# The first branch's output adds on GpSimd, its last two units without GpSimd pairs, and the sums of down weights two units later

## The chip, the cores and the metric

The kernel runs on one core of a Trainium2 chip. The metric is the device time of one execution in microseconds (us); less is better. The engines that a core has are named as in the profile: PE (TensorE, the matrix engine), DVE (VectorE), ACT (ScalarE), POOL (GpSimd) and SP (SyncE, which here only issues DMAs). Each works through its own queue of instructions in order: an instruction that waits holds back all that stand behind it on its engine.

## The reference

One layer of a diffusion backbone over 1024 latent tokens and 256 context tokens, with a model width of 1024. What matters here is the attention; cut to its core:

```python
# A: 8 heads, windowed (+-128) with a sink logit; B: 8 heads, global. Both also see all 256 context keys.
def _sink_softmax(scores, sink):
    m = jnp.maximum(jnp.max(scores, axis=-1, keepdims=True), sink)
    e = jnp.exp(scores - m)
    return e / (jnp.sum(e, axis=-1, keepdims=True) + jnp.exp(sink - m))

out_a = _gqa_values(_sink_softmax(scores_a, sink), v_blk)      # per block of 128 queries
out_b = _gqa_values(jax.nn.softmax(scores_b, axis=-1), v_all)
merged = (g_a * (out_a @ w_branch_a) + g_b * (out_b @ w_branch_b)) @ w_out
```

Ahead of it stand the modulation and the projections to queries, keys, values and gates; behind it a LayerNorm, a SwiGLU feed-forward network with a convolution (weights up, gate and down), and a second LayerNorm.

## The kernel before, in words

The result has to be good to fp32, so the kernel splits fp32 operands in two parts that PE can take fast: a high part (a cast, line L83 or L81 on the helper `split`) and a low part (a subtraction, L86), and multiplies them as two or three matmuls that add up.

The stages in order: modulation and projections (to about 335 us), attention (to about 760 us), merge and output projection, the up and gate projections, the down projection. The down projection uses sums of blocks of the down weights; these sums are made in DRAM by DMAs alone, during the attention.

**Attention** is cut into 32 units. Unit `u` is a branch (0: windowed, units 0 to 15; 1: global, units 16 to 31), a block `i` of 128 queries and one of two groups `g` of four heads; the program's names carry it as `0_4_1` (branch, block, group). For each unit there are these steps:

- `qprep` (L476 to L488), two units ahead: POOL splits the queries into `qs` (L83, L86; one buffer for all units), PE transposes them (`qtr`, L483), ACT copies them out (L486), two DMAs swap halves.
- scores: for each head two or more matmuls into `s` (L493, L494; L528 adds the window's mask), then DVE's maximum (L538) and ACT's exponential (L505); `norm` (L562 to L573) ends the row sums `sm`.
- `rows` (L577 to L588): PE transposes the row sums (`str`), and three DMAs spread them over partitions (`rb`).
- values, one unit behind: for each key tile `n`, PE transposes the probabilities (`ptr`, L614), and they are split into `pth` and `ptl`. Most tiles go to ACT (the cast, L623) and DVE (the subtraction, L624). Tile 3 of each unit of branch 0, and tiles 2 and 6 of branch 1 (`POOL_LO`), are "pooled": ACT copies the tile to SBUF (`prw`, L620) and POOL does the cast and the subtraction (L83, L86). Then PE multiplies both parts with the values (`av`, L635 and L636).
- output, `out_step` (L638 to L655): ACT copies `av` to SBUF (`avs`, L641), POOL moves its upper half down (`up`, L643), two adds of 64x256 make `ot` (L647), POOL multiplies by `rb` (L650) and splits the result into `O` (L83, L86). The two adds run on DVE for branch 0 and for the last unit, on POOL for branch 1.

The loop over units at the end of the phase interleaves these steps; the order in which instructions stand on each engine is then set by a scheduler that weighs them with costs of its own. Branch projections (`fill`) are mixed in from unit 18 on. At the end of nine of the units, a table `DNS` calls `wd_sums`: SP loads a block of down weights into a DRAM tile `sd` (L683), and POOL issues a DMA that adds another block onto it (L685). It is POOL that waits there until the first has landed. Twelve such adds stand on POOL, in units 16 to 28. The sums are read much later, in the down projection.

Of the kernel before, what the change touches and what calls it, by code (L numbers as in the profile page):

```python
# [10 lines left out]
ALU = mybir.AluOpType  # L11
# [7 lines left out]
NT = 8  # L19
# [9 lines left out]
POOL_LO = (3,), (2, 6)  # L29
# [32 lines left out]
VOFF = 0.0  # L62
VSPAN = 1.0
VSC = 0, 1
DNS = {u0 + 2 * n + (u0 == 20): (n, j0, j1) for u0, j0, j1 in ((16, 0, 4), (20, 4, 8), (24, 8, 11)) for n in range(3)}


@with_exitstack
def layer_kernel(
# [6 lines left out]
    nc = tc.nc  # L76
    PSUM = bass.MemoryType.PSUM

    def split(src, hi, lo, hi_eng, lo_eng):
        if hi_eng is nc.scalar:  # L80
            nc.scalar.copy(hi, src)  # L81
        elif hi_eng is nc.gpsimd:
            nc.gpsimd.tensor_scalar(out=hi, in0=src, scalar1=1.0, scalar2=0.0, op0=ALU.mult, op1=ALU.add)  # L83
        else:
            hi_eng.tensor_copy(hi, src)
        lo_eng.tensor_tensor(out=lo, in0=src, in1=hi.bitcast(F32), op=ALU.subtract)  # L86
# [376 lines left out]
    class Unit:  # L463
# [141 lines left out]
        def value_steps(self):  # L605
            nm, kt = self.id, self.kt
            vh = self.br * 2 + self.g
            last = self.id == f"1_{NT - 1}_1"
            parts = {}

            def tr_step(n):
                tr = pt_tile(f"ptr{nm}_{n}")
                for h in range(4):
                    nc.tensor.transpose(tr[:, h * P:(h + 1) * P], self.pslice(h, n), ident)  # L614
                hi = att.tile([P, 512], R32, tag="pth", name=f"pth{nm}_{n}", bufs=4)
                lo = att.tile([P, 512], R32, tag="ptl", name=f"ptl{nm}_{n}", bufs=4)
                pooled = n in POOL_LO[self.br] and not last
                if pooled:
                    rw = att.tile([P, 512], F32, tag="ptr", name=f"prw{nm}_{n}", bufs=2)
                    nc.scalar.copy(rw, tr)  # L620
                    split(rw, hi, lo, nc.gpsimd, nc.gpsimd)
                else:
                    nc.scalar.copy(hi, tr)  # L623
                    nc.vector.tensor_tensor(out=lo, in0=tr, in1=hi.bitcast(F32), op=ALU.subtract)  # L624
                parts[n] = hi, lo
                return pooled

            def av_step(n):
                first = self.left == len(kt)
                self.left -= 1  # L630
                if first:
                    self.av = ps2.tile([P, 512], F32, tag="av", name=f"av{nm}")
                hi, lo = parts.pop(n)
                v = VT[kt[n] // 2][:, kt[n] % 2, vh]
                nc.tensor.matmul(self.av, v, hi, start=first, stop=False)  # L635
                nc.tensor.matmul(self.av, v, lo, start=False, stop=self.left == 0)  # L636

            def out_step():  # L638
                av = self.av
                avs = att.tile([P, 512], F32, tag="ptr", name=f"avs{nm}", bufs=2)  # L640
                nc.scalar.copy(avs, av)  # L641
                up = att.tile([HD, 512], F32, tag="up", name=f"up{nm}", bufs=1)
                nc.gpsimd.tensor_scalar(out=up, in0=avs[HD:P], scalar1=1.0, scalar2=0.0, op0=ALU.mult, op1=ALU.add)  # L643
                ot = att.tile([P, 2, P], F32, tag="ot", name=f"ot{nm}", bufs=1)
                oe = nc.gpsimd if self.br and not last else nc.vector
                for h in range(2):
                    oe.tensor_tensor(out=ot[h * HD:(h + 1) * HD],  # L647
                                     in0=avs[0:HD].rearrange("p (a b q) -> p a b q", b=2, q=P)[:, :, h],
                                     in1=up.rearrange("p (a b q) -> p a b q", b=2, q=P)[:, :, h], op=ALU.add)
                nc.gpsimd.tensor_tensor(out=ot, in0=ot, in1=self.rb, op=ALU.mult)  # L650
                hf = self.i // 4
                qs = slice((self.i % 4) * P, (self.i % 4 + 1) * P)
                split(ot, otile(self.br, hf, 0, self.g)[:, :, qs], otile(self.br, hf, 1, self.g)[:, :, qs],
                      nc.gpsimd, nc.gpsimd)

            def step(ns):
                pooled = [tr_step(n) for n in ns]
                for n, pl in zip(ns, pooled):
                    clk[0] += 1
                    avq.append((self, n, clk[0] + LAG[self.br] + (PLAG[self.br] if pl else 0)))  # L660
                    av_issue()

            self.left = len(kt)
            self.av_step, self.out_step = av_step, out_step
            g = 1 + self.br
            steps = [lambda n=n: step(range(n, n + g)) for n in range(0, len(kt), g)]
            steps.insert(3 if self.br else 2 if self.i else len(steps), self.rows)
            return steps

    tokens = []  # L670
    sd = {}

    def wd_sums(n, j0, j1):
        def a(r, c):
            return w_dn[c * NH + j0:c * NH + j1][:, :, 4 * r:4 * r + 4].rearrange("n p f q -> p n (f q)")

        def put(key, src, *more):
            tag = tokens.pop()
            t = dpool.tile([P, j1 - j0, HALF], F32, tag=tag, name=f"sd{key}_{j0}")
            for j in range(j0, j1):  # L680
                sd[key, j] = t[:, j - j0]
            sd[key] = t
            nc.sync.dma_start(t, src)  # L683
            for m in more:
                nc.gpsimd.dma_start(t, m, accum_op=ALU.add)  # L685

        if n == 0:
            put(1, a(1, 0), a(1, 1))
            put(3, a(0, 0), a(1, 0))
        elif n == 1:  # L690
            put(2, sd[1], a(0, 0))
        else:
            put(4, sd[2], a(0, 1))
# [130 lines left out]
    for n, (gi, k) in enumerate(order):  # L824
# [8 lines left out]
        if gi == "g":  # L833
            for hf in (0, 1):
                last = gate(k, hf)
# [50 lines left out]
    def otile(br, hf, hl, g):  # L886
        key = br, hf, hl, g
        if key not in O:
            O[key] = opool.tile([P, 2, HALF], R32, tag="O", name="O%d%d%d%d" % key, bufs=12)
        return O[key]  # L890
# [4 lines left out]
    def pt_tile(name, dt=F32):  # L895
        return ps2.tile([P, 512], dt, tag="pt", name=name, bufs=3)
# [17 lines left out]
    def av_issue(flush=False):  # L914
        while avq:
            u = avq[0][0]
            c = [e for e in avq if e[0] is u and (flush or e[2] <= clk[0])]
            if not c:
                return
            e = min(c, key=lambda e: e[2])  # L920
            avq.remove(e)
            u.av_step(e[1])
            if u.left == 0:
                u.out_step()
# [36 lines left out]
    def done(br, i, g):  # L961
        if g and i % 2:
            hput(f"Q{br}_{i - 1}")
        if g and i == NT - 1:
            hput(f"KL{br * 2}", f"KL{br * 2 + 1}")
# [4 lines left out]
    for u in range(nu + 1):  # L970
        vs, fs = [], []
        while vq and (vq[0] <= u - VL or vq[0] >= 16 or u >= 17):
            vs += units[vq.pop(0)].value_steps()
        ss = []
        if u < nu:
            ss = units[u].score_steps()
            if u + 2 < nu:
                ss.append(units[u + 2].qprep)
        if u == 31:
            first = branch_steps(1, w_b, (0, 1), att, (nc.gpsimd, nc.gpsimd), (0,))  # L980
            first[0]()
        for hf, (u0, u1) in enumerate(FILL):
            if u == u0:
                fill += branch_steps(0, w_a, (hf,), att, (nc.gpsimd, nc.gpsimd))
                ends = [n * (u1 - u0) / len(fill) for n in range(len(fill))]
            if u0 <= u < u1:
                fs = [fill.pop(0) for e in ends if u - u0 <= e < u - u0 + 1]
        if u < nu:
            ss = [units[u].context] + ss
        seq = []  # L990
        for lst, of, sp in ((ss, 0.0, SPAN[u >= 17]), (vs, VOFF, VSPAN), (fs, 0.0, 1.0)):
            for n, st_ in enumerate(lst):
                seq.append((of + sp * (n + 0.5) / len(lst), st_))
        for _, st_ in sorted(seq, key=lambda e: e[0]):
            st_()
        if u in DNS:
            wd_sums(*DNS[u])
        if u < nu:
            vq.append(u)
            done(units[u].br, units[u].i, units[u].g)  # L1000
# [86 lines left out]
    for f in range(2, KT):  # L1087
# [4 lines left out]
        for hs in halves:  # L1092
            n = HALF * len(hs)
# [239 lines left out]
    for f in (4, 6):  # L1333
        for si in (1, 2):
# [3 lines left out]
            elif f == 6:  # L1338
                (_, st), (_, dg), (_, ca), *ap = ln1(si)
                n = len(pend) - 4  # L1340
# [584 lines left out]
```

## Time and profile before

| What | Value |
|---|---|
| time, median of 3 runs | 1562.94 us (1562.52 to 1565.55) |
| time of the execution that was profiled | 1565.22 us |
| span of that execution in the profile | 1563.4 us |
| mean granted clock of PE | 0.995 of full speed |
| busy: PE, DVE, ACT, POOL | 98%, 76%, 52%, 50% of the span |
| attention | about 335 to 760 us |

How to read it: a row of the timeline has the start in us, the busy time in us, engine, line, operation, what it writes and reads, and how many instructions run together; in brackets stands how long the engine sat idle before it and which instruction released it. A row of a table of windows has, for each engine, its busy time in that stretch, then the granted clock of PE, the share of time in which the DMA engines were busy, and what they moved in GB/s. The times of one execution differ from the median of the runs by some us, so what the change adds or takes is worked out within the profiled execution.

### The profile page before, as it was taken

Reading aid. Unit: us, or ns where it says so; the run is one execution under the profiler, and the core shown is the slowest. Engines: PE = TensorE matmul, PEld = TensorE weight load, DVE = VectorE, ACT = ScalarE, POOL = GpSimd, SP = SyncE. Lnnn points to the kernel's source line nnn. Section 1 sums busy time; section 2 is a strip of 40 time slices with the busy share of each in tenths; the row PEclk is TensorE's granted clock in tenths of the full one; section 3 lists DMA queues with packets and bytes.
Section 4 is the critical chain, followed back from the end, with each engine's and each line's share of the span. In section 5 each row is a group of like instructions: output and inputs, shape, how many; then the busy total and the mean of one; then the engine's idle time right before and its main releaser. Section 6 shows DMA issues by size and latency. Waiting matters only on the chain.

```text
span 1563.4 us, 22286 instructions
## 1 busy us (share of the span) xinstructions
PE 1531.6 (98%) x7804; PEld 1282.2 (82%) x7804; DVE 1187.6 (76%) x1714; ACT 808.6 (52%) x1431; POOL 782.2 (50%) x795
## 2 busy tenths in 40 slices
PE   9999999999999999999999999999999999999997
PEld 7888888888877877877888997888888888888887
DVE  6677976548887777777774788888888888657884
ACT  5322223358887777777431673544444444435552
POOL 0356422526666777776332455666677764121121
PEclk9999999999999999999999999999999999999998
DMA  9776662322235666631550223233334446996721
GB/s 371 267 239 239 207 245 92 106 84 66 65 116 137 150 149 151 148 80 35 180 184 16 98 79 120 81 112 115 120 102 114 113 117 191 363 265 212 251 103 55
DMA packets 113105, 232.11 MB, mean 148 GB/s; under 512 B 13056, under 2 KB 27904, under 8 KB 112896
## 3 DMA queue, kind: packets, MB, share of 16 engines
q1 hardware_dynamic: 97760, 201.82, 38.4%
q0 software_dynamic: 10400, 20.19, 8.3%
q10 hardware_dynamic: 4832, 8.68, 1.5%
q8 instruction: 61, 1.00, 0.3%
q14 instruction: 52, 0.43, 0.1%
HBM read 179.45 MB, written 65.86 MB: 157 GB/s over the span
## 4 chain that ended last, share of the span: by engine, by line
PE 54%; DVE 3%; ACT 1%; issue 1%; POOL 0%; DVEq 0%; ACTq 0%
PE p L89 4%; PE p L90 4%; PE p L91 4%; PE b L89 2%; PE b L91 2%; PE b L90 2%; PE c L89 2%; PE c L91 2%; PE d L91 2%; PE d L89 2%; PE c L90 2%; PE d L90 2%; PE a L91 2%; PE a L89 2%; PE a L90 2%; PE y L91 2%
## 5 line engine op out<-in xcount | busy, mean ns | idle before, releaser
L624 DVE TENSOR_TENSOR ptl<-ptr,pth 128x512 fp32r<-128x512 f32 x190 | 126.2, 682 | 32.6 <-ACT pth L623 32.2
L623 ACT CAST pth<-ptr 128x512 fp32r<-128x512 f32 x190 | 108.0, 593 | 54.0 <-PE ptr L614 32.6
L86 DVE TENSOR_TENSOR ld<-rd,hd 128x1024 fp32r<-128x1024 f32 x77 | 94.9, 1249 | 50.2 <-ACT hd L81 48.1
L505 ACT ACTIVATE p<-p,nm 128x1024 f32<-128x1024 f32 (+2 forms) x128 | 125.9, 985 | 4.5 <-DVE p L538 4.3
L614 PE MATMUL ptr<-ident,p 128*128 128x128 f32 x816 | 122.4, 277 | 4.4 <-DVE ptl L624 3.2
L81 ACT CAST hd<-rd 128x1024 fp32r<-128x1024 f32 x77 | 79.5, 1050 | 81.1 <-PE p L91 55.1
L614 PEld LDWEIGHTS ptr<-ident,p 128*128 128x128 f32 x816 | 94.1, 141 | 25.6 <-DVE ptl L624 7.9
L86 POOL TENSOR_TENSOR wlg<-wg,whg 128x512 fp32r<-128x512 f32 x32 | 47.7, 1500 | 123.3 <-ACT whg L81 123.3
L635 PE MATMUL av<-pth,VT 128*128 128x512 f32 x236 | 104.6, 443 | 2.1 <-ACT avs L641 1.5
L89 PE MATMUL p<-hd 128*128 128x512 f32 x264 | 103.2, 391 | 0.0
L91 PE MATMUL p<-hd,ld 128*128 128x512 f32 x264 | 102.7, 389 | 0.0
L90 PE MATMUL p<-ld,hd 128*128 128x512 f32 x264 | 102.7, 389 | 0.0
L636 PE MATMUL av<-ptl,VT 128*128 128x512 f32 x236 | 98.1, 416 | 2.7 <-POOL ptl L86 2.7
L89 PE MATMUL g<-hh,whg 128*128 128x512 f32 x256 | 99.9, 390 | 0.0
L91 PE MATMUL g<-hh,wlg 128*128 128x512 f32 x256 | 99.7, 389 | 0.0
L90 PE MATMUL g<-hl,whg 128*128 128x512 f32 x256 | 99.6, 389 | 0.0
L538 DVE TENSOR_SCALAR_CACHE_REDUCE p<-s,cvt,nmc 128x1024 f32<-128x1024 f32 x64 | 83.2, 1316 | 8.8 <-PE s L494 7.7
L493 PE MATMUL s<-KL,q 128*128 128x512 f32 (+2 forms) x192 | 75.6, 394 | 5.3 <-ACT p_x L505 2.8
L787 ACT ACTIVATE sg<-g,bgc 128x512 f32<-128x512 f32 x32 | 22.0, 686 | 96.1 <-PE g L91 96.1
L494 PE MATMUL s<-KL,q 128*128 128x512 f32 (+2 forms) x192 | 71.6, 373 | 0.0
L81 ACT CAST wS<-s 128x512 fp32r<-128x512 f32 x76 | 45.3, 620 | 46.4 <-POOL s L1227 45.7
L81 ACT CAST wA<-ru 128x512 fp32r<-128x512 f32 x57 | 35.5, 623 | 62.4 <-PE d L91 33.8
(436 smaller groups left out, 5015.2 us busy)
## 6 DMA issues: line engine op xcount, KB each, us to landing
wml<-in_wmodT_dram SPq DMA_DIRECT2D x48, 512.0 KB
ru<-in_w_up_dram SPq DMA_DIRECT2D x38, 512.0 KB
rd<-td SPq DMA_DIRECT2D x55, 256.0 KB
rd<-sd SPq DMA_DIRECT2D x44, 256.0 KB
rd<-in_w_dn_dram SPq DMA_DIRECT2D x33, 256.0 KB
wm<-in_wmodT_dram SPq DMA_DIRECT2D x16, 512.0 KB
wg<-in_w_g_dram SPq DMA_DIRECT2D x32, 256.0 KB
sgd<-sg ACTq DMA_DIRECT2D x32, 256.0 KB
```

The source lines that it names most:

```text
L81: nc.scalar.copy(hi, src)
L86: lo_eng.tensor_tensor(out=lo, in0=src, in1=hi.bitcast(F32), op=ALU.subtract)
L89: nc.tensor.matmul(ps, a[0], b[0], start=start, stop=False, skip_group_check=resumed)
L90: nc.tensor.matmul(ps, a[0], b[1], start=False, stop=False, skip_group_check=resumed)
L91: nc.tensor.matmul(ps, a[1], b[0], start=False, stop=stop, skip_group_check=resumed)
L505: nc.scalar.activation(p, s, AF.Exp, bias=nm[:, h:h + 1], scale=scale, accum_out=sm[:, h:h + 1])
L538: nc.vector.tensor_scalar(out=p, in0=o, scalar1=self.qscale(nqs)[:, hs] if self.br else -1.0, scalar2=self.other[:, hs], op0=ALU.mult, op1 ...
L614: nc.tensor.transpose(tr[:, h * P:(h + 1) * P], self.pslice(h, n), ident)
L623: nc.scalar.copy(hi, tr)
L624: nc.vector.tensor_tensor(out=lo, in0=tr, in1=hi.bitcast(F32), op=ALU.subtract)
L635: nc.tensor.matmul(self.av, v, hi, start=first, stop=False)
L636: nc.tensor.matmul(self.av, v, lo, start=False, stop=self.left == 0)
```

## The change

Four edits, all in the attention phase:

1. `pooled` is false for block 7 of branch 0 (its last two units, `0_7_0` and `0_7_1`). Their tile 3 goes to ACT and DVE like the others.
2. The two adds into `ot` (L647) run on POOL for every unit but the last. Before, the 16 units of branch 0 had them on DVE.
3. `DNS` calls `wd_sums` two units later: at units 18, 20, 22, 23, 25, 27, 26, 28 and 30.
4. The accumulating DMAs are no longer issued in `wd_sums` at once, but put on a list, and issued on POOL at the end of the next unit.

```diff
-DNS = {u0 + 2 * n + (u0 == 20): (n, j0, j1) for u0, j0, j1 in ((16, 0, 4), (20, 4, 8), (24, 8, 11)) for n in range(3)}
+DNS = {u0 + 2 * n + (u0 == 22): (n, j0, j1) for u0, j0, j1 in ((18, 0, 4), (22, 4, 8), (26, 8, 11)) for n in range(3)}
...
-                pooled = n in POOL_LO[self.br] and not last
+                pooled = n in POOL_LO[self.br] and not last and self.id[:3] != f"0_{NT - 1}"
...
-                oe = nc.gpsimd if self.br and not last else nc.vector
+                oe = nc.vector if last else nc.gpsimd
...
+    adds = []
...
-            for m in more:
-                nc.gpsimd.dma_start(t, m, accum_op=ALU.add)
+            adds.extend((t, m) for m in more)
...
+        while adds:
+            t, m = adds.pop(0)
+            nc.gpsimd.dma_start(t, m, accum_op=ALU.add)
         if u in DNS:
             wd_sums(*DNS[u])
```

The scheduler gives several engines another order for it. On POOL, in the middle of branch 0, this is one cycle of before, from the query split of unit 0_4_1 to that of 0_5_0 (`qs` the split queries, `up`, `ot` and `O` the output of unit 0_2_0, `pth` and `ptl` the pooled tile 3 of unit 0_2_1):

```order
L83 TENSOR_SCALAR qs0_4_1_3957<-Q0_4_1588 128x4x64
L643 TENSOR_SCALAR up0_2_0_3812<-avs0_2_0_3810 64x512
L86 TENSOR_TENSOR qs0_4_1_3957<-Q0_4_1588,qs0_4_1_3957 128x4x64
L83 TENSOR_SCALAR pth0_2_1_3_3843<-prw0_2_1_3_3845 128x512
L650 TENSOR_TENSOR ot0_2_0_3814<-ot0_2_0_3814,rb0_2_0_3650 128x256
L86 TENSOR_TENSOR ptl0_2_1_3_3844<-prw0_2_1_3_3845,pth0_2_1_3_3843 128x512
L83 TENSOR_SCALAR O0000_3305<-ot0_2_0_3814 128x2x128
L86 TENSOR_TENSOR O0010_3306<-ot0_2_0_3814,O0000_3305 128x2x128
L83 TENSOR_SCALAR qs0_5_0_4089<-Q0_4_1588 128x4x64
```

And this is the same cycle on POOL after the change:

```order
L83 TENSOR_SCALAR qs0_4_1_3957<-Q0_4_1588 128x4x64
L643 TENSOR_SCALAR up0_2_0_3812<-avs0_2_0_3810 64x512
L86 TENSOR_TENSOR qs0_4_1_3957<-Q0_4_1588,qs0_4_1_3957 128x4x64
L647 TENSOR_TENSOR ot0_2_0_3814<-avs0_2_0_3810,up0_2_0_3812 64x256 x2
L650 TENSOR_TENSOR ot0_2_0_3814<-ot0_2_0_3814,rb0_2_0_3650 128x256
L83 TENSOR_SCALAR O0000_3305<-ot0_2_0_3814 128x2x128
L86 TENSOR_TENSOR O0010_3306<-ot0_2_0_3814,O0000_3305 128x2x128
L83 TENSOR_SCALAR pth0_2_1_3_3843<-prw0_2_1_3_3845 128x512
L86 TENSOR_TENSOR ptl0_2_1_3_3844<-prw0_2_1_3_3845,pth0_2_1_3_3843 128x512
L83 TENSOR_SCALAR qs0_5_0_4089<-Q0_4_1588 128x4x64
```

The two adds are new, and the pooled pair `pth`, `ptl` has gone from the middle of the cycle to its end, behind the whole output of the unit before. Ten cycles in a row, from the output of unit 0_1_0 to that of 0_5_1, stand like this; behind them come two cycles of another order.

On PE, before, the part of the same cycle from the use of the first pooled part (`pth0_2_1_3`) to the transpose of the next queries (`qtr0_4_1`) is this, `ptr` being transposes of unit 0_3_0 and `s` scores of unit 0_3_1:

```order
L635 MATMUL av0_2_1_3849<-pth0_2_1_3_3843,VT4_2139 128x512
L614 MATMUL ptr0_3_0_2_3929<-ident_58,p0_3_0_0_3750 128x128
...
L636 MATMUL av0_2_1_3849<-ptl0_2_1_3_3844,VT4_2139 128x512
L635 MATMUL av0_2_1_3849<-pth0_2_1_4_3857,VT4_2139 128x512
L493 MATMUL s0_3_1_2_3903<-KL1_2131,q10_3_1_3701 128x384
...
L636 MATMUL av0_2_1_3849<-ptl0_2_1_4_3858,VT4_2139 128x512
L483 MATMUL qtr0_4_1_3960<-identr_59,qs0_4_1_3957 128x128 x4
```

After the change the same instructions stand so:

```order
L635 MATMUL av0_2_1_3849<-pth0_2_1_3_3843,VT4_2139 128x512
L636 MATMUL av0_2_1_3849<-ptl0_2_1_3_3844,VT4_2139 128x512
L614 MATMUL ptr0_3_0_2_3929<-ident_58,p0_3_0_0_3750 128x128
...
L635 MATMUL av0_2_1_3849<-pth0_2_1_4_3857,VT4_2139 128x512
L636 MATMUL av0_2_1_3849<-ptl0_2_1_4_3858,VT4_2139 128x512
L483 MATMUL qtr0_4_1_3960<-identr_59,qs0_4_1_3957 128x128 x4
```

The five score matmuls of `s0_3_1_2` now stand ahead of `str0_3_0` and `pth0_2_1_3`; between the use of `ptl0_2_1_3` and the query transposes only four transposes and two matmuls are left. In both orders `qtr0_4_1` stands behind the use of the pooled low part.

On POOL, where branch 0 ends, before: the output of unit 0_7_0 with a DMA add (`sd1_0`) inside it, that of 0_7_1 behind it, and among them pooled pairs of branch 1:

```order
L643 TENSOR_SCALAR up0_7_0_5172<-avs0_7_0_5170 64x512
L685 DMA sd1_0_5183<-in_w_dn_dram 512x1x512
L650 TENSOR_TENSOR ot0_7_0_5174<-ot0_7_0_5174,rb0_7_0_4974 128x256
L83 TENSOR_SCALAR pth1_0_0_2_5244<-prw1_0_0_2_5246 128x512
L83 TENSOR_SCALAR O0100_4346<-ot0_7_0_5174 128x2x128
L86 TENSOR_TENSOR O0110_4347<-ot0_7_0_5174,O0100_4346 128x2x128
L86 TENSOR_TENSOR ptl1_0_0_2_5245<-prw1_0_0_2_5246,pth1_0_0_2_5244 128x512
L643 TENSOR_SCALAR up0_7_1_5263<-avs0_7_1_5261 64x512
L650 TENSOR_TENSOR ot0_7_1_5265<-ot0_7_1_5265,rb0_7_1_5112 128x256
```

And after, from the same instruction on:

```order
L643 TENSOR_SCALAR up0_7_0_5146<-avs0_7_0_5144 64x512
L647 TENSOR_TENSOR ot0_7_0_5148<-avs0_7_0_5144,up0_7_0_5146 64x256 x2
L650 TENSOR_TENSOR ot0_7_0_5148<-ot0_7_0_5148,rb0_7_0_4974 128x256
L83 TENSOR_SCALAR O0100_4346<-ot0_7_0_5148 128x2x128
L86 TENSOR_TENSOR O0110_4347<-ot0_7_0_5148,O0100_4346 128x2x128
...
L83 TENSOR_SCALAR pth1_0_0_2_5234<-prw1_0_0_2_5236 128x512
L643 TENSOR_SCALAR up0_7_1_5253<-avs0_7_1_5251 64x512
L86 TENSOR_TENSOR ptl1_0_0_2_5235<-prw1_0_0_2_5236,pth1_0_0_2_5234 128x512
```

No DMA add stands there any more, and ahead of this piece the pooled pair of unit 0_7_1 is gone from POOL too.

## The prediction

> **What bounds the kernel now.** I read the page first, for the busy shares:
>
> ```profile
> PE 1531.6 (98%) x7804; PEld 1282.2 (82%) x7804; DVE 1187.6 (76%) x1714; ACT 808.6 (52%) x1431; POOL 782.2 (50%) x795
> ```
>
> PE is the bound. Work that moves between the other engines counts only where PE waits for it, and POOL, at 50%, looks free. A share over the whole span says little, so I cut the attention into stretches with the table of windows:
>
> ```profile
> 390.00:420.00 30.00, 29.99 (x203) 25.89 (x202) 25.87 (x63) 27.29 (x66) 19.27 (x29) 1.00 0.25 67
> 465.00:500.00 35.00, 31.12 (x171) 24.28 (x170) 26.21 (x42) 26.45 (x60) 22.94 (x36) 0.95 0.59 129
> 482.08:485.49 3.41, 1.22 (x6) 0.72 (x7) 2.30 (x5) 0.00 (x0) 2.13 (x5) 1.00 1.07 195
> 485.49:488.90 3.41, 3.41 (x16) 2.92 (x17) 3.41 (x6) 2.01 (x4) 3.21 (x5) 0.50 0.02 4
> ```
>
> After each stretch's length stand the busy times of PE, its weight loads, DVE, ACT and POOL, then the granted clock. In the middle of branch 0 (390 to 420) PE has no gap. Where branch 0 hands over to branch 1 (465 to 500) PE loses some 4 us to waits, and right after a stretch with PE busy 1.22 of 3.41 us, it runs 3.41 us at half clock. So the change can win at the handover, and in branch 0 it can only lose. What it would lose there I looked up in one cycle of POOL's timeline:
>
> ```profile
> 399.45 0.41 POOL L83 TENSOR_SCALAR qs<-Q 128x256 fp32r<-128x256 f32 x1 [1.46 <-PE qtr L483]
> 399.94 0.61 POOL L643 TENSOR_SCALAR up<-avs 64x512 f32<-64x512 f32 x1
> 400.63 0.74 POOL L86 TENSOR_TENSOR qs<-Q,qs 128x256 fp32r<-128x256 f32 x1
> 402.42 0.62 POOL L83 TENSOR_SCALAR pth<-prw 128x512 fp32r<-128x512 f32 x1 [1.04 <-ACT prw L620]
> 403.00 0.74 POOL L650 TENSOR_TENSOR ot<-ot,rb 128x256 f32<-128x256 f32 x1
> 403.70 1.29 POOL L86 TENSOR_TENSOR ptl<-prw,pth 128x512 fp32r<-128x512 f32 x1
> 404.96 0.40 POOL L83 TENSOR_SCALAR O<-ot 128x256 fp32r<-128x256 f32 x1
> 405.44 0.74 POOL L86 TENSOR_TENSOR O<-ot,O 128x256 fp32r<-128x256 f32 x1
> 407.66 0.41 POOL L83 TENSOR_SCALAR qs<-Q 128x256 fp32r<-128x256 f32 x1 [1.48 <-PE qtr L483]
> ```
>
> A cycle takes 407.66 − 399.45 = 8.21 us, and POOL idles 1.48 + 1.04 = 2.5 us of it. PE's part of the same cycle:
>
> ```profile
> 405.20 0.66 PE L614 MATMUL ptr<-ident,p 128*128 128x128 f32 x4
> 405.62 0.48 PE L636 MATMUL av<-ptl,VT 128*128 128x512 f32 x1
> 405.94 0.40 PE L635 MATMUL av<-pth,VT 128*128 128x512 f32 x1
> 406.17 0.34 PE L493 MATMUL s<-KL,q 128*128 128x384 f32 x1
> ...
> 406.88 0.39 PE L636 MATMUL av<-ptl,VT 128*128 128x512 f32 x1
> 407.11 0.46 PE L483 MATMUL qtr<-identr,qs 128*128 128x128 f32 x4
> ```
>
> The `ptl` of 403.70 is done at 404.99, and PE takes it at 405.62, after 0.63 us of slack and without a wait. There is a ring: POOL's cast into `qs` waits for `qtr` of the unit before (one buffer), `qtr` stands in PE's queue behind the use of `ptl`, and `ptl` stands in POOL's queue behind the cast. Its length sets a floor under the cycle. Now it is 403.70 + 1.29 − 399.45 = 5.54 us on POOL plus 407.66 − 405.62 = 2.04 on PE and back, 7.6 in all, against the 8.2 of PE's own work. It does not bind.
>
> **The change part by part.** *Adds on POOL, branch 0.* What they cost per instruction, from the rows of their line:
>
> ```profile
> L647 DVE TENSOR_TENSOR ot<-avs,up x34: 388/418/862, 353.3 to 758.4; 64x256 f32<-64x256 f32 x34
> L647 POOL TENSOR_TENSOR ot<-avs,up x30: 717/732/755, 500.1 to 750.8; 64x256 f32<-64x256 f32 x30
> ```
>
> DVE saves 2 × 0.418 = 0.84 us a unit, which is worth nothing where PE has no gap. POOL pays 2 × 0.732 = 1.46. By busy time that fits into the 2.5 us of idle; but the new order puts both adds, the multiplication and the split of `O` ahead of the pooled pair, so all of it goes into the ring. Branch 1 already has this piece, in the same order:
>
> ```profile
> 500.07 1.52 POOL L647 TENSOR_TENSOR ot<-avs,up 64x256 f32<-64x256 f32 x2
> ...
> 504.38 1.30 POOL L86 TENSOR_TENSOR ptl<-prw,pth 128x512 fp32r<-128x512 f32 x1
> ```
>
> From the first add to the end of `ptl` it is 504.38 + 1.30 − 500.07 = 5.61 us. Ahead of it stand the cast, `up` and the low part of `qs`: 400.63 − 399.45 = 1.18, and about 0.70 from the start of the last to the next start (as 403.70 − 403.00 for an instruction as long). That is 7.49 on POOL. On PE the five score matmuls (406.88 − 406.17 = 0.71) are gone from behind `ptl`, and four transposes (405.62 − 405.20 = 0.42) stand there instead: 2.04 − 0.71 + 0.42 = 1.75. I add 0.06 for the hand from POOL to PE, which now waits (at 464.63 below). The ring is 7.49 + 0.06 + 1.75 = 9.30 us, so the cycle grows by 9.30 − 8.2 = 1.1, as a wait of PE for `ptl`. The ten cycles in the new order run, in the trace of before, from
>
> ```profile
> 366.26 0.41 POOL L83 TENSOR_SCALAR qs<-Q 128x256 fp32r<-128x256 f32 x1 [0.98 <-PE qtr L483]
> ...
> 440.44 0.41 POOL L83 TENSOR_SCALAR qs<-Q 128x256 fp32r<-128x256 f32 x1 [1.46 <-PE qtr L483]
> 449.45 0.41 POOL L83 TENSOR_SCALAR qs<-Q 128x256 fp32r<-128x256 f32 x1 [2.29 <-PE qtr L483]
> ```
>
> to the last of these (eight rows left out). The tenth takes 449.45 − 440.44 = 9.01 us already and hides most of the ring; the nine ahead of it, (440.44 − 366.26) / 9 = 8.24 each, pay: 9 × 1.10 = **+9.9**. If POOL ran gapless (7.07 us, the sum of the busy times in these rows with the adds), the ring would be 8.88 and the term +6; a ring of 9.4 gives +11. The tenth and the cycle behind it, which has another order: 0 to +1.1, taken as **+0.5**, the middle, no row being nearer.
>
> The Trainium skill's "GPSIMD Engine Reference", section "Engine selection", gives elementwise adds of two inputs to VectorE, with GpSimd about two times slower: it speaks against this edit. The rows here have 0.732 against 0.418, 1.75 times; by the page's factor two adds would be 1.67 instead of 1.46 us, and the term, by that estimate, +11.8.
>
> *The start of branch 0.* There the adds on DVE do hold PE up once:
>
> ```profile
> 353.30 0.42 DVE L647 TENSOR_TENSOR ot<-avs,up 64x256 f32<-64x256 f32 x1 [2.67 <-POOL up L643]
> ...
> 354.60 0.27 PE L577 MATMUL str<-ident,sm 128*4 128x128 f32 x1 [1.08 <-DVE sm L573]
> 355.28 0.44 PE L493 MATMUL s<-KL,q 128*128 128x384 f32 x1 [0.42 <-DVE p L538]
> ```
>
> DVE stood behind `up`, and the row sums and a maximum behind it. Without the adds the 1.08 + 0.42 us go: **−1.5**, at worst 0 if POOL, now with the adds, is late for something else there.
>
> *The handover: no pairs of units 14 and 15, no DMA adds, no adds on DVE.* PE, POOL and DVE of that stretch:
>
> ```profile
> 464.63 0.50 PE L636 MATMUL av<-ptl,VT 128*128 128x512 f32 x1 [1.44 <-POOL ptl L86]
> 482.47 0.50 PE L636 MATMUL av<-ptl,VT 128*128 128x512 f32 x1 [0.62 <-POOL ptl L86]
> 484.77 1.64 PE L614 MATMUL ptr<-ident,p 128*128 128x128 f32 x8 [1.80 <-DVE ptl L624]
> ...
> 477.40 1.18 POOL L685 DMA_DIRECT2D sd<-in_w_dn_dram  x1 [1.89 <-DMA sd<-in_w_dn_dram]
> ...
> 482.50 0.61 POOL L643 TENSOR_SCALAR up<-avs 64x512 f32<-64x512 f32 x1
> ...
> 483.15 0.85 DVE L647 TENSOR_TENSOR ot<-avs,up 64x256 f32<-64x256 f32 x2 [3.38 <-POOL up L643]
> 484.03 1.29 DVE L624 TENSOR_TENSOR ptl<-ptr,pth 128x512 fp32r<-128x512 f32 x2
> ```
>
> This is a chain: POOL waits 1.89 us for a block of down weights and issues the add for 1.18; 3.07 us late, `ptl` comes 0.62 too late for PE; `up` stands behind it, DVE waits 3.38 for `up`, two `ptl` stand behind that, and PE waits 1.80. The wait at 464.63 is for the pair of unit 0_7_0. All three have lost their cause: 1.44 + 0.62 + 1.80 = 3.86. The half clock behind them costs 3.41 / 2 = 1.7 more and should not come, since the share of 1.22 in 3.41 that stands ahead of it rises. Together −5.6 if nothing else gets late. Something will: the two pairs go to DVE and ACT (the low part is 1.29 us for two there, and 26.21 of 35 us were busy), and POOL's adds come before its first pairs of branch 1. I keep four fifths, **−4.5**; the bounds are −5.6 and −2.
>
> The Trainium skill's "TensorE: Matmul & The Clock Gate", section "What's actually happening", has the clock fall after a window of about 3.4 us in which PE idles. The trace shows 0.50 for just 3.41 us, but behind a window with 1.22 us of work, so here it was not a whole window without work. By the page's words the fall had a cause that the change need not touch, and this term would be −2.8.
>
> *The sums in units 18 to 30.* Moved, not removed. Their rows on POOL:
>
> ```profile
> L685 POOL DMA_DIRECT2D sd<-in_w_dn_dram x12: 1085/1122/1375, 465.7 to 692.3; - x12
>   DMA sd<-in_w_dn_dram: 3.6, 2
> ```
>
> The twelve cost POOL 1.12 us each before and after; the waits for loads (3.6 us in two places) shrink, as a unit now lies between load and add. What stands behind a waiting add on POOL is its pooled pairs, for which PE waits; only the one at 477.40 was seen to reach PE (above). SP's loads are issued as before, two units later, and what they make is read only in the down projection, long after the attention. **0 ± 1**.
>
> *Sum.* +9.9 + 0.5 − 1.5 − 4.5 + 0 = **+4.4 us**, so the profiled execution's 1565.22 would be 1569.6, and the median, 2.28 lower, 1562.94 + 4.4 = **1567.3**.
>
> **The rivals.** *POOL's slack takes the adds (faster).* The cycle stays at 8.2 and only the gains are left: 0 − 1.5 − 4.5 = −6, 1556.9. It speaks for it that POOL would be busy 7.2 of 8.2 us. The point that decides: the stretch from the cast to the end of `ptl` must be at most 8.2 − 1.75 − 0.06 = 6.39 us, 1.1 less than I count and less than the 7.07 of its instructions alone, unless PE reaches `qtr` by less than 1.75. I see no room for that, but I take these rows from two places of the trace, and the ring's closing depends on the one buffer of `qs`. 0.2.
>
> *The ring binds half as hard (no change).* If the instructions abut better and each cycle grows by 0.5 to 0.7, a loss of 4.5 to 6.3 with the +0.5 behind it meets gains of 6: −1 to +0.8, about 1563. It speaks for it that the gapless sum gives +6. 0.24.
>
> *The half clock stays (slower still).* If at the handover another wait lets PE work only a third of some window, the 3.41 us at 0.50 come again, and the sum is 1.7 higher: +6.1, 1569.0. Against it: no pooled pair and no DMA add of POOL's is left at that place. The Trainium skill's rule above would give the same, for another reason. 0.1.
>
> *The ring's waits bring the clock down (much slower).* A wait of 1.1 us in 9.3 leaves PE busy 88%. The fall came behind 36%, and the 1.44 us at 464.63 brought none. Once a cycle it would cost 9 × 1.7 = +15, 1583. 0.02.
>
> *The forecast* itself: 0.44.
>
> **How the numbers follow.** A measurement of this kernel can tell about 0.2% from no change, 3.1 us. Slower holds the forecast and the two cases with the clock, 0.56, less 0.04 for a forecast that comes out under 3.1 us: 0.52. Same: those 0.04 and 0.21 of the half-hard ring, 0.25. Faster: the slack and the rest of the half-hard ring, 0.23. The low end is the slack's 1556.9. For the high end I take the ring at +11, the cycle behind at +1.1, −1.5 and −2 for the gains, and 1 for the sums: +9.6, 1572.5. Within the slower cases but the last it is 1566 to 1572.5.
>
> **What would show it.** In the trace of after: between 366 and 450 the casts into `qs` some 9.3 us apart, POOL without idle time between them but for one wait for `qtr`, and PE waiting 1 us a cycle at L636 for POOL's `ptl`; no such waits and 8.2 us would make me wrong at the main step. At the handover no half clock, no wait for `sd` on POOL, and PE waiting under 1.2 us in all; the end of attention some 4 us later. If the start still shows 1.08 at `str`, that term is wrong. If the loss is in branch 1 (500 to 760), the cause is one that I priced at nothing.

## The result, and the profile after

| Kernel | Median | Ratio to before, 95% interval |
|---|---|---|
| before (6 runs) | 1563.43 us | |
| the change (6 runs) | 1568.63 us | 1.0033 [1.0020, 1.0046] |

The change makes the kernel slower by about 5.2 us, 3.1 to 7.2. The profiled execution of after has a span of 1567.7 us, 4.3 more than before's 1563.4. The page's first row and the table of windows, for the same stretches as in the prediction and for two around 740 us (columns as there):

```profile
PE 1534.7 (98%) x7804; PEld 1284.0 (82%) x7804; DVE 1177.2 (75%) x1684; ACT 807.9 (52%) x1431; POOL 806.4 (51%) x823
```

```profile
390.00:420.00 30.00, 26.88 (x175) 22.58 (x173) 21.63 (x51) 22.93 (x55) 22.68 (x33) 1.00 0.21 58
465.00:500.00 35.00, 34.41 (x212) 27.80 (x213) 30.54 (x53) 31.24 (x75) 27.16 (x46) 1.00 0.31 95
...
736.50:739.91 3.41, 1.75 (x9) 1.18 (x9) 2.43 (x5) 2.90 (x10) 0.45 (x1) 1.00 1.08 195
739.91:743.33 3.42, 3.42 (x13) 2.92 (x12) 2.56 (x4) 3.37 (x6) 2.60 (x4) 0.50 0.02 3
```

The shares of the page have hardly moved. The windows have: in the middle of branch 0 PE now loses 3.1 of 30 us where it lost nothing, at the handover it loses 0.6 of 35 where it lost 3.9, and the half clock of 3.41 us is gone from 485 us and has come at 739.9. One cycle of POOL after the change, and PE's use of the pooled low part in it:

```profile
403.46 0.41 POOL L83 TENSOR_SCALAR qs<-Q 128x256 fp32r<-128x256 f32 x1 [1.84 <-PE qtr L483]
...
405.35 1.53 POOL L647 TENSOR_TENSOR ot<-avs,up 64x256 f32<-64x256 f32 x2
...
409.67 1.27 POOL L86 TENSOR_TENSOR ptl<-prw,pth 128x512 fp32r<-128x512 f32 x1
412.79 0.41 POOL L83 TENSOR_SCALAR qs<-Q 128x256 fp32r<-128x256 f32 x1 [1.84 <-PE qtr L483]
```

```profile
411.00 0.50 PE L636 MATMUL av<-ptl,VT 128*128 128x512 f32 x1 [0.85 <-POOL ptl L86]
```

POOL's work of a cycle has no gap but the wait for `qtr`, and PE waits 0.85 us for `ptl`. The cycle is 412.79 − 403.46 = 9.33 us. It consists of 409.67 + 1.27 − 403.46 = 7.48 on POOL, 0.06 to PE, and 412.79 − 411.00 = 1.79 on PE and back.

To see where the 4.3 us come from, I compare the starts of like instructions, here POOL's casts into `qs`, in after:

```profile
366.10 0.41 POOL L83 TENSOR_SCALAR qs<-Q 128x256 fp32r<-128x256 f32 x1 [0.55 <-PE qtr L483]
...
450.15 0.41 POOL L83 TENSOR_SCALAR qs<-Q 128x256 fp32r<-128x256 f32 x1 [1.85 <-PE qtr L483]
459.05 0.40 POOL L83 TENSOR_SCALAR qs<-Q 128x256 fp32r<-128x256 f32 x1 [1.41 <-PE qtr L483]
469.19 0.40 POOL L83 TENSOR_SCALAR qs<-Q 128x256 fp32r<-128x256 f32 x1 [1.86 <-PE qtr L483]
...
510.74 0.41 POOL L83 TENSOR_SCALAR qs<-Q 128x256 fp32r<-128x256 f32 x1 [0.90 <-PE qtr L483]
```

and in before, where the counterparts of the last two are

```profile
457.87 0.40 POOL L83 TENSOR_SCALAR qs<-Q 128x256 fp32r<-128x256 f32 x1 [0.89 <-PE qtr L483]
...
506.57 0.41 POOL L83 TENSOR_SCALAR qs<-Q 128x256 fp32r<-128x256 f32 x1 [0.89 <-PE qtr L483]
```

Later on I take waits that PE has in both traces, first before, then after:

```profile
744.95 0.33 PE L614 MATMUL ptr<-ident,p 128*128 128x128 f32 x1 [0.48 <-DVE ptl L624]
...
971.20 0.47 PE L89 MATMUL c<-T13h,wS 128*128 128x512 f32 x1 [1.75 <-DVE c L1390]
```

```profile
750.32 0.33 PE L614 MATMUL ptr<-ident,p 128*128 128x128 f32 x1 [0.48 <-DVE ptl L624]
...
975.45 0.47 PE L89 MATMUL c<-T13h,wS 128*128 128x512 f32 x1 [0.63 <-DVE c L1393]
```

| Stretch (term) | after's lead or lag at its end | what the stretch cost | predicted |
|---|---|---|---|
| start of branch 0, to 366 | −0.16 | −0.2 | −1.5 |
| nine cycles, to before's 440.44 | +9.71 | +9.9 | +9.9 |
| tenth cycle and the one behind it, to 457.87 | +11.32 | +1.6 | +0.5 |
| handover, to 506.57 | +4.17 | −7.2 | −4.5 |
| branch 1, to 744.95 | +5.37 | +1.2 | 0 |
| rest, to 971.20 and the end | +4.25, +4.3 | −1.1 | not named |

The last row is no work of the change as far as the runs show: this wait at the wide matmuls was 1.75 us in before and 0.63 in after; in the twelve kernels below it was 0.62 to 0.64 in nine, 1.75 in two and 2.03 in one.

The marks are POOL's casts, and PE's queue stands in another order around two of them, so some of PE's work falls into another row of the table. Up to the first mark PE does 145 matmuls in before and 140 in after; the five that it does later are score matmuls of one head, 0.71 us by the rows of the prediction:

```profile
343.90:366.26 22.36, 20.86 (x145) 18.54 (x145) 18.11 (x45) 17.98 (x45) 14.03 (x20) 1.00 0.24 55
...
343.90:366.10 22.20, 20.65 (x140) 17.75 (x140) 16.94 (x41) 17.29 (x43) 16.88 (x25) 1.00 0.23 55
```

And ahead of the handover's first mark, six matmuls `s_x` (scores with the context) stand behind the query transposes in before (first two rows) and ahead of them in after (last two rows, 468.64 − 467.85 = 0.79 us):

```profile
457.24 0.54 PE L483 MATMUL qtr<-identr,qs 128*128 128x128 f32 x4
457.91 0.39 PE L493 MATMUL s_x<-KC,q 128*128 128x256 f32 x1
...
467.85 0.36 PE L493 MATMUL s_x<-KC,q 128*128 128x256 f32 x1
...
468.64 0.45 PE L483 MATMUL qtr<-identr,qs 128*128 128x128 f32 x4
```

For like work the start cost about +0.5 instead of −0.2, the nine cycles +9.2, the two behind them +0.8 and the handover −6.4. The sum stays the same.

### The profile page after: what moved, and what is told of

Its sections match the earlier page's. It is cut to its first block, busy times and chain, and to the rows that moved or that the text cites. A ratio compares the mean times of both kernels' runs of the same rounds, so it can differ in the third digit from the quotient of the medians.

```text
span 1567.7 us, 22275 instructions
## 1 busy us (share of the span) xinstructions
PE 1534.7 (98%) x7804; PEld 1284.0 (82%) x7804; DVE 1177.2 (75%) x1684; ACT 807.9 (52%) x1431; POOL 806.4 (51%) x823
## 4 chain that ended last, share of the span: by engine, by line
PE 54%; DVE 3%; ACT 1%; issue 1%; POOL 0%; DVEq 0%; ACTq 0%
PE p L89 4%; PE p L91 4%; PE p L90 4%; PE b L89 2%; PE b L90 2%; PE b L91 2%; PE c L89 2%; PE c L90 2%; PE d L90 2%; PE c L91 2%; PE d L91 2%; PE d L89 2%; PE a L90 2%; PE a L91 2%; PE a L89 2%; PE y L89 2%
```

## The experiments

The theory is the prediction's: a ring of waits through POOL and PE, made longer by the adds. Its rivals were that POOL is too slow or disturbs DVE, whatever the order, and that the other edits account for the time. Four kernels take the change apart, four alter one thing in it each (buffers, the lag, the units whose adds move), three follow what those showed, and one puts together what helped.

| Kernel | Median, us | Ratio to before, 95% interval |
|---|---|---|
| 1 all but the adds | 1557.50 | 0.9968 [0.9955, 0.9981] |
| 2 adds alone | 1572.78 | 1.0065 [1.0050, 1.0080] |
| 3 pairs alone | 1562.94 | 0.9998 [0.9989, 1.0007] |
| 4 sums alone | 1561.24 | 0.9988 [0.9978, 0.9998] |
| 5 two buffers of `qs` | 1570.82 | 1.0050 [1.0035, 1.0065] |
| 6 lag 2 | 1564.81 | 1.0010 [1.0000, 1.0020] |
| 7 a buffer for one unit's row sums | 1570.62 | 1.0048 [1.0033, 1.0063] |
| 8 adds on POOL in block 7 only | 1558.15 | 0.9967 [0.9958, 0.9976] |
| 9 kernel 1, last sum earlier | 1558.00 | 0.9963 [0.9950, 0.9975] |
| 10 lag 2 and more row-sum buffers | 1554.57 | 0.9942 [0.9926, 0.9957] |
| 11 branch weights in halves | 1565.01 | 1.0009 [1.0000, 1.0018] |
| 12 all that helped | 1550.68 | 0.9917 [0.9904, 0.9931] |

**1. All but the adds.** The changed kernel with

```diff
-                oe = nc.vector if last else nc.gpsimd
+                oe = nc.gpsimd if self.br and not last else nc.vector
```

> The changed kernel with the adds of branch 0 back on DVE (pairs of the last two units off POOL and later sums kept). Theory (ring of query split, pooled pair and query transposes, lengthened by POOL's adds): the query splits between 366 and 450 us stand 8.2 us apart again, PE has no wait for POOL's ptl there, and what remains are the gains of the other edits: 1556 to 1560 us. Rival (the loss comes from POOL's adds holding up DVE's small operations, or from the edits of pairs and sums): then it stays above 1563, or the cycles stay above 8.5 us.

The casts into `qs`, nine cycles apart:

```profile
366.69 0.41 POOL L83 TENSOR_SCALAR qs<-Q 128x256 fp32r<-128x256 f32 x1 [0.97 <-PE qtr L483]
...
440.98 0.41 POOL L83 TENSOR_SCALAR qs<-Q 128x256 fp32r<-128x256 f32 x1 [1.45 <-PE qtr L483]
```

That is 8.25 us a cycle, before's 8.24, and the kernel beats before by 0.2 to 0.45%. The loss is the adds' and the rest of the change is a gain.

**2. The adds alone.** The kernel before with the line of `oe` from the change.

> The kernel before with the adds of branch 0 on POOL and nothing else. Theory: cycles of 9.3 us in nine cycles, +10 us by 450 us; at the handover POOL still has the pairs and the DMA adds as well, so nothing is gained there: 1572 to 1577 us. Rival (the handover gains come from DVE being free of the adds): about the changed kernel's 1568.

```profile
366.21 0.41 POOL L83 TENSOR_SCALAR qs<-Q 128x256 fp32r<-128x256 f32 x1 [0.54 <-PE qtr L483]
...
450.44 0.41 POOL L83 TENSOR_SCALAR qs<-Q 128x256 fp32r<-128x256 f32 x1 [1.85 <-PE qtr L483]
```

The cycles are (450.44 − 366.21) / 9 = 9.36 us, and 1572.78 lies where the theory had it. At the handover PE now waits for POOL, 1.71 and 1.11 us around 493 us, and the half clock comes behind it, at 494.4. The lag on before is 10.0 us at 450 us and still 10.0 at 562.5 (before: 552.5), so DVE's freedom from the adds alone gained no more at the handover than the two cycles ahead of it lost.

**3. The pairs alone, and 4. the sums alone.** The kernel before with the line of `pooled`, and with `DNS`, the list `adds` and its loop.

> The kernel before with only the pooled pairs of units 14 and 15 given to ACT and DVE. Theory by my sum: the waits of 1.44 and perhaps 0.62 us for POOL's ptl go, the chain behind the DMA add stays: 1560.5 to 1562.5 us. Rival (POOL's relief also ends the chain and the half clock): 1557 to 1559.

> The kernel before with only the sums of down weights two units later and their adds a unit behind. Theory: POOL's 3.07 us at the handover and with it the waits of 0.62 and 1.80 us and the half clock go, and a DMA add moves out from between p_x and the low part of branch weights near 547 us (1.0 us) and another one into such a place near 733 us: 1557 to 1561 us. Rival (the pairs alone made the handover late): within 2 us of 1563.

In the pairs' kernel PE's 1.44 us at 464.6 are gone, but 20 us on POOL has to wait for its block of weights all the longer, since it comes there sooner, and PE with it:

```profile
477.66 1.19 POOL L685 DMA_DIRECT2D sd<-in_w_dn_dram  x1 [3.57 <-DMA sd<-in_w_dn_dram]
```

```profile
484.43 0.33 PE L614 MATMUL ptr<-ident,p 128*128 128x128 f32 x1 [3.16 <-DVE ptl L624]
```

The 1.80 us of before are 3.16 here, and the half clock stays, at 484.86. What one wait gives the next one takes: no difference, and the median misses the theory's range by 0.4 us. In the sums' kernel the same wait is 0.59 us and no half clock follows there (one comes at 732.1), a gain of 0.02 to 0.22%. Its median lies just above the theory's range and within the rival's; what decides is the trace, in which the chain behind the DMA add is gone and the waits of 1.42, 0.62 and 0.53 us remain. Apart they gave −0.3 and −2.0 us by medians, together (kernel 1) −5.8: each edit removes a wait that otherwise takes up what the other one saved.

**5. Two buffers of split queries.** The changed kernel with

```diff
-            qs = qp.tile([P, 4, P], R32, tag="qs", name=f"qs{nm}", bufs=1)
+            if not self.br and self.i:
+                qs = att.tile([P, 8, P], R32, tag="whl", name=f"qs{nm}", bufs=2)[:, 0:4]
+            else:
+                qs = qp.tile([P, 4, P], R32, tag="qs", name=f"qs{nm}", bufs=1)
```

> The changed kernel with a second buffer for the split queries of branch 0 (units from block 1 on), adds still on POOL. Theory (a ring that is closed by the one buffer): POOL may cast the next queries without the query transposes of the unit before, so POOL runs ahead, the waits of 0.85 us for ptl go and the cycles fall from 9.34 to 8.2 us: 1557 to 1561 us. Rival (POOL's rate, or its reach for SBUF beside DVE, sets the cycle, whatever the buffers): cycles stay above 9 us and the time above 1566.

```profile
405.03 0.41 POOL L83 TENSOR_SCALAR qs<-Q 128x256 fp32r<-128x256 f32 x1 [1.85 <-PE qtr L486]
```

```profile
403.23 0.50 PE L639 MATMUL av<-ptl,VT 128*128 128x512 f32 x1 [0.86 <-POOL ptl L86]
```

Nothing opened: the cycle is 9.34 us still. The order shows why. The scheduler used the second buffer to put the cast a whole unit earlier on POOL, ahead of unit 0_1_1's output where it had stood ahead of 0_2_0's. There it waits for the transposes of two units before, and these stand behind the use of `ptl` just as before. So "closed by the one buffer" was wrong. What closes the ring is the place in two in-order queues: a cast that waits for `qtr`, with the pair behind it on POOL, and `qtr` behind the pair's use on PE.

**6. Lag 2.** The changed kernel with `PLAG = 2, 2`, so that PE uses the pooled tile one step later, behind `qtr`.

> The changed kernel with the lag of branch 0's pooled tile raised from 1 to 2: PE uses the pooled pair one step later, behind the query transposes, and the scheduler puts the pair ahead of the adds on POOL; POOL's work per unit is the same. Theory (ring): the pair is no longer ahead of the query transposes, the ring is open, cycles of 8.2 us: 1556 to 1560 us. Rival (rate): above 9 us per cycle still.

PE doesn't wait for `ptl` any more, with the same work on POOL. The casts are 8.99 us apart on average, and in every second cycle PE has another wait:

```profile
409.58 0.33 PE L614 MATMUL ptr<-ident,p 128*128 128x128 f32 x1 [1.56 <-ACT rb L583]
```

```profile
409.27 0.26 ACT L583 COPY rb<-str 4x128 f32<-4x128 f32 x1 [1.83 <-POOL ot L650]
```

ACT copies a unit's row sums into one of two buffers `rb`, and must wait until POOL has multiplied by the sums that lie in it; PE's transposes stand behind that. The time falls by 3.8 us against the change, less than half of what the theory had: behind the ring stands a second limit, and it takes most of the gain.

**7. A buffer for one unit's row sums.** The same wait stands once in the changed kernel, at the start, so there I gave unit 0_1_0 a buffer of its own:

```diff
+            if self.id in ("0_1_0",):
+                self.rb = att.tile([P, 8, P], F32, tag="wraw", name=f"rb{self.id}", bufs=1)[:, 0:2]
+            else:
-            self.rb = att.tile([P, 2, P], F32, tag="rb", name=f"rb{self.id}", bufs=2)
+                self.rb = att.tile([P, 2, P], F32, tag="rb", name=f"rb{self.id}", bufs=2)
```

> The changed kernel with a buffer of its own for the spread row sums of unit 0_1_0. Theory (ACT's copy of the row sums waits for POOL's multiplication, which the adds made late, and PE for ACT): the wait of 1.02 us before PE's transposes near 364.6 us goes and the first cast into qs behind it comes 1 us earlier; the ring is untouched: 1567 to 1568.5 us. Rival (POOL itself is late there, the copy only the messenger): no change near 366 us, 1568.6.

The wait goes, and the cast of 366.10 comes at 363.14. But the buffer is borrowed from the branch weights, and the scheduler drew their split (1.05 and 2.40 us on POOL, behind 1.71 us of waiting for the load) into the cycle that starts there; the next two casts are 12.69 and 10.20 us on, PE waits 3.15 us for `pth` at 382.03, a half-clock stretch follows at 383.9, and the lead is gone: the median is 2 us above the change's, where a gain of up to 1.6 was expected. It shows what the wait was; whether the start could keep the gain, it does not.

**8. Adds on POOL in block 7 only.** As in kernel 1, with POOL for the last two units of branch 0:

```diff
+                oe = nc.vector if last or (not self.br and self.i < NT - 1) else nc.gpsimd
```

> The changed kernel with the adds on POOL only in block 7, the last two units of branch 0 (DVE has them in units 0 to 13). Theory: no ring in 366 to 450 us, and at the handover DVE is free of four adds and of their wait for up: 1 us or less against the kernel with all of branch 0's adds on DVE, so 1556.5 to 1558.5 us. Rival (POOL is the late one at the handover): 1558.5 to 1561.

1558.15 against 1557.50, with intervals that overlap: that it matters at the handover who adds, the runs don't show.

**9. The last sum a unit earlier.** Kernel 1 with the DMA adds of unit 30 in unit 29. This one rests on three places in the traces of before and after. After, around 734 us, POOL, DVE and PE:

```profile
733.46 1.08 POOL L998 DMA_DIRECT2D sd<-in_w_dn_dram  x1
734.13 2.81 POOL L86 TENSOR_TENSOR lwb<-rwb,hwb 128x1024 fp32r<-128x1024 f32 x1
```

```profile
734.33 2.65 DVE L551 TENSOR_TENSOR nmc<-nmc,cvt 128x4 f32<-128x4 f32 x1
```

```profile
737.64 0.33 PE L614 MATMUL ptr<-ident,p 128*128 128x128 f32 x1 [1.06 <-DVE ptl L624]
```

A DVE operation on 128x4 values lasts 2.65 us and ends at 736.98, POOL's subtraction at 736.94. Before, without the DMA add in that place, they ended at 732.65 and 732.64:

```profile
730.24 2.40 POOL L86 TENSOR_TENSOR lwb<-rwb,hwb 128x1024 fp32r<-128x1024 f32 x1
```

```profile
730.97 1.68 DVE L551 TENSOR_TENSOR nmc<-nmc,cvt 128x4 f32<-128x4 f32 x1
```

So each DMA add that stands between the two parts of a weight split puts DVE off by about a microsecond (2.54 us before and 2.65 after with such an add, 1.42 to 1.68 without). The change took one such add away near 547 us (before had 0.96 us of PE's waiting there) and put one in at 733.

> The kernel with the adds of branch 0 on DVE (first experiment) and the last of the sums one unit earlier, in unit 29 instead of 30, so that no DMA add stands between the high and the low part of the second branch's weights on POOL. Theory (DVE's multiplication of 128x4 is held until POOL's subtraction of 128x1024 ends, and the DMA add puts that end off by 1 us): the wait of 1.1 us near 728 us falls to 0.1, and 1 us less than the first experiment: 1556 to 1557.5 us. Rival (the wait comes from DVE's own queue): no change there, 1557.5.

The wait near 728 us is gone, and at the end of attention this kernel is 1.3 us ahead of kernel 1 in their traces; the median, 1558.00, shows nothing of it. In these two traces two things behind the attention take the lead back: the wait at the wide matmuls is 1.75 us where kernel 1 has 0.63, and a half-clock stretch stands at 843 us where kernel 1 has none. The mechanism is shown, its worth in the whole time is not.

**10. Lag 2 and more buffers of row sums.** Kernel 6, with every third unit of branch 0 in a buffer of its own:

```diff
+            if not self.br and (2 * self.i + self.g) % 3 == 2:
+                self.rb = att.tile([P, 8, P], F32, tag="wraw", name=f"rb{self.id}", bufs=1)[:, 0:2]
+            else:
```

> The changed kernel with lag 2 for branch 0's pooled tile and, for every third unit of branch 0, another buffer for the spread row sums, so that ACT's copy needn't wait for POOL's multiplication of two units before. Theory (with the ring open, the two buffers of row sums are what is left): PE's 1.56 us every second cycle go, cycles of 8.2 us with all adds on POOL: 1556 to 1561 us. Rival (POOL, at 7.1 of 8.2 us, can't keep up in any order): cycles stay at 8.9 or more on average, 1564 or more.

```profile
363.18 0.41 POOL L83 TENSOR_SCALAR qs<-Q 128x256 fp32r<-128x256 f32 x1
...
436.92 0.42 POOL L83 TENSOR_SCALAR qs<-Q 128x256 fp32r<-128x256 f32 x1
```

(436.92 − 363.18) / 9 = 8.19 us a cycle, with every add on POOL: the rival of rate is refuted. Between 394 and 413 us PE has no wait at all. The kernel is 14.1 us faster than the change, by the order on two engines and a buffer.

**11. Branch weights in halves.** The changed kernel with POOL's subtraction for the branch weights (called through `split` in `branch_steps`) as two of 128x512:

```diff
+            for q in (slice(0, 4), slice(4, 8)):
+                nc.gpsimd.tensor_tensor(out=l[:, q], in0=r[:, q], in1=h[:, q].bitcast(F32), op=ALU.subtract)
```

> The changed kernel with POOL's subtraction for the branch weights in two halves of 128x512. Theory (DVE's 128x4 multiplication with both inputs in SBUF starts only when POOL's running subtraction ends): near 734 us it ends with the first half, so it takes 1.4 us or less instead of 2.65, PE's wait of 1.06 us and the half clock behind it go: 1 to 2 us less, 1566.5 to 1568 us. Rival (it waits for its input or for the queue): 2.6 us still, 1568.6.

At the place that I had named, it fails:

```profile
730.36 1.75 POOL L939 TENSOR_TENSOR lwb<-rwb,hwb 128x512 fp32r<-128x512 f32 x1
...
730.36 2.98 POOL L939 TENSOR_TENSOR lwb<-rwb,hwb 128x512 fp32r<-128x512 f32 x2
```

```profile
730.56 2.80 DVE L551 TENSOR_TENSOR nmc<-nmc,cvt 128x4 f32<-128x4 f32 x1
```

The halves run without a gap, from 730.36 to 733.34, and DVE ends at 733.36, with the second one; PE waits 1.25 us at 734 us, where it was 1.06. At three others it holds, for instance:

```profile
550.31 1.29 POOL L939 TENSOR_TENSOR lwb<-rwb,hwb 128x512 fp32r<-128x512 f32 x1
```

```profile
551.29 0.33 DVE L551 TENSOR_TENSOR nmc<-nmc,cvt 128x4 f32<-128x4 f32 x1
```

Here DVE comes in at 551.62 as the first half ends at 551.60, where in after the same operation took 1.43 us. PE's waits for ACT of 0.60 us go at three places, and the kernel is 3.6 us faster than the change, more than I had expected from the one place. About a microsecond of that is not shown to be the edit's: the half clock that follows the wait of 1.06 us in after does not come here, behind one of 1.25. Why DVE did not get in between the halves at 732 us, where POOL had issued a DMA just ahead of them, stays open.

**12. All that helped.** Kernel 10 with the halves of 11 and the earlier last sum of 9.

> The version that the runs point to: the changed kernel with lag 2 and the third buffer of row sums (open ring, adds on POOL), POOL's subtraction for the branch weights in two halves, and the last of the sums in unit 29. If the gains add: 1554.6 less 1.1 us each at three places of the second branch and 1 near the end: 1550 to 1552 us. Rival (other waits take their place, or the half-clock stretches move): 1553.5 to 1555.

```profile
390.00:420.00 30.00, 29.91 (x204) 26.17 (x203) 24.67 (x55) 25.96 (x63) 25.31 (x37) 1.00 0.26 67
465.00:500.00 35.00, 33.78 (x201) 27.37 (x200) 28.25 (x46) 29.59 (x65) 31.75 (x50) 1.00 0.62 163
```

1550.68 us: 0.7 to 1% faster than before and 18 us faster than the change, with PE full in branch 0 while POOL works 25.3 of 30 us.

## Why the prediction was right, point by point

**The ring.** Forecast 9.30 us a cycle, measured 9.33 to 9.34; +9.9 for nine cycles, measured +9.9. That the nine cycles agree to the decimal is luck. The forecast took 8.2 us off each ring, and not the 8.24 that it had itself for the nine on average, which gives 9 × 1.06 = 9.5. Measured, the first cycle grew by 0.7 only, since before has 8.61 us there (366.26 to 374.87), and the eight others by 1.14 each. Of these 1.14, 0.85 stand as PE's wait for `ptl`; the rest stands as busy time of PE, 8.47 us a cycle instead of 8.20. Both pieces that I put together from two places of the trace came out: 7.49 on POOL (7.48) and 1.75 on PE (1.79). Kernels 1, 2 and 10 show that it is the adds, in this order, and not POOL's rate. One part of the reason was wrong: the ring doesn't hang on the one buffer of `qs` (kernel 5), but on where the pair and `qtr` stand.

**The cycles behind it.** +0.5 was the middle of two bounds, 0 and +1.1, for want of a row; measured +1.6, above the upper bound, but 0.8 of it is the work of the six `s_x` matmuls, which the handover lost; for like work it is +0.8, within the bounds. The first of the two cost nothing, as forecast (8.90 us against 9.01). In the second PE waits for another pair that now stands behind POOL's adds:

```profile
465.07 0.50 PE L635 MATMUL av<-pth,VT 128*128 128x512 f32 x1 [1.00 <-POOL pth L83]
```

I had read the order there only so far as to see that it was another.

**The start.** −1.5 forecast, −0.2 measured. The 1.08 and 0.42 us did go, but another wait came, 10 us on:

```profile
364.58 0.33 PE L614 MATMUL ptr<-ident,p 128*128 128x128 f32 x1 [1.02 <-ACT rb L583]
```

```profile
364.27 0.26 ACT L583 COPY rb<-str 4x128 f32<-4x128 f32 x1 [1.40 <-POOL ot L650]
```

The failing step is "without the adds the 1.08 + 0.42 us go": I followed who had waited for DVE, and not who would wait for POOL's later multiplication through the two buffers of `rb`. By the marks the bound of 0 held; for like work the start cost about +0.5, which is beyond it.

**The handover.** −4.5 forecast, −7.2 measured by the marks and −6.4 for like work, beyond the bound of −5.6. The chain was right, link by link: no wait for a block of weights, no half clock, and PE's only wait there above 0.4 us is one of 0.42. Too small was the list: before had two more waits of PE between 457 and 507 us, 0.62 for ACT's `q` and 0.53 for DVE's maximum, which I had not counted, and the discount of a fifth for "something will get late" was not needed. The forecast's 3.86 and 1.7 with these two, less the 0.42, are 6.3. Kernels 3 and 4 show that the edits pay together and hardly alone.

**The sums in branch 1.** 0 ± 1 forecast, +1.2 measured, in two halves of opposite sign: the DMA add that moved away from the weight split at 547 us gave back 1.06 us, the one that moved into the split at 733 cost about 1.2 (lag 3.08 at after's 681.98, 4.33 at 739.36), and the half clock at 739.9 about 1.0 more. That half clock is not a sure price of the wait: kernels 1 and 7 have the same wait of 1.11 us with 0.60 behind it, and no half clock there. I had asked whether POOL waits for the adds. The price lay in what they put off on POOL, for DVE.

So the sum, +4.4 against +4.3 in the profiled execution and +5.2 by the medians, came, by the marks, from one term that was exact and four errors that cancel: +1.3, +1.1, −2.7 and +1.2, with −1.1 from a wait outside the change. For like work no term was exact: the errors are +2.0 at the start, −0.7 in the nine cycles, +0.3, −1.9 and +1.2, and the same −1.1. The ring was foreseen; that the total came so near was luck. The rival "POOL's slack takes the adds" is refuted by the trace of after, "binds half as hard" too, and "the ring's waits bring the clock down" by the granted clock of 1.00 from 390 to 420 us. "The half clock stays" was nearer than I gave it credit for: it left the handover, and one came 250 us later, behind another wait.

## What to carry to other kernels

An engine's idle time says whether work fits, and nothing about where in its queue it will stand. Before moving work to an engine that looks half free, follow the queue in the new order from a wait round to itself and add up the ring; here 1.5 us into 2.5 us of idle time cost 1.1 a cycle, and the same work in another order cost nothing. More buffers are no cure by themselves, since a scheduler may spend them on issuing earlier. And two edits that remove waits in the same stretch should be tried together before either is thrown away.

## What the hardware showed beyond that

A small DVE operation with both inputs in SBUF is held while POOL runs a subtraction. The rows of L551, in the kernel with halves (minimum, median and maximum in ns):

```profile
L551 DVE TENSOR_TENSOR nmc<-nmc,cvt x16: 147/272/2801, 470.7 to 730.6; 128x4 f32<-128x4 f32 x16
```

The same operation takes 0.15 or 2.80 us, and in the long cases it ended within 0.04 us of POOL's. The Trainium skill's "GPSIMD Engine Reference", section "Specifications", says that GpSimd shares SBUF interfaces with VectorE and contends with VectorE instructions of two SBUF inputs; the rows agree and give the size: DVE's operation lasts until POOL's running instruction ends, and in the one case of kernel 11 until the end of two in a row.

PE's clock fell to 0.50 for 3.41 us behind windows in which PE had been busy 1.22 (before) and 1.75 (after) of 3.41 us. The Trainium skill's "TensorE: Matmul & The Clock Gate", section "What's actually happening", lets the clock fall after an idle window of that length; here a window that was half idle was enough, and the measurement decides. Busy time alone does not foretell the fall either. The first two rows are of before, where it follows a window with PE busy for 3.24 us (16 of the 23 matmuls are of one column, 128x1); the last is of kernel 1, which keeps the full clock through two waits, of 1.11 and 0.60 us, like those ahead of 739.9 in after:

```profile
847.31:850.72 3.41, 3.24 (x23) 2.77 (x22) 1.20 (x4) 0.00 (x0) 0.34 (x2) 1.00 0.01 2
850.72:854.13 3.41, 3.41 (x10) 2.63 (x9) 1.37 (x3) 0.00 (x0) 0.85 (x1) 0.50 0.02 5
...
720.00:740.00 20.00, 17.50 (x105) 13.87 (x103) 16.31 (x22) 13.22 (x30) 14.44 (x19) 1.00 0.38 77
```

What decides it stays open, so whether a half clock comes can't be forecast from these rows.
